# Values of the second and third attention group projected in natural token order, ahead of the queries, and brought into dilated order through DRAM

## The chip, the cores and the metric

The program runs on one core of one Trainium2 chip. The metric is the device time of one execution in microseconds (us). Three executions of the kernel before took 1969.75, 1970.76 and 1972.15 us (median 1970.76).

## What is computed

One layer of a hybrid decoder, for a prompt of 1024 tokens and for 8 decode tokens with the same weights: an input projection `h @ w_in`, a dilated attention of three head groups, a retention of four heads, gates, an output projection and a feed-forward block. The change touches the dilated attention of the prompt. Cut to that:

```python
DILATED_PATTERNS = ((128, 1), (512, 4), (2048, 16))      # (window, dilation) of the three groups
h = x * (1 + scale1) + shift1
qa, ka, va, ... = split(h @ w_in)                        # va: 3 groups x 4 heads x 64 = 3 x 256 columns
for g, (window, dil) in enumerate(DILATED_PATTERNS):
    o, lse = _dilated_group_prompt(qa[g], ka[g], va[g], window, dil)   # tokens i and j meet only if i % dil == j % dil
    keep = min(window, 1024)
    outputs += [ka[g][-keep:], va[g][-keep:]]            # prompt_k, prompt_v, in token order
```

The outputs `prompt_k` and `prompt_v` hold the last 128, 512 and 1024 tokens of the three groups, in natural token order.

## The kernel before, in words

`h` lies transposed in SBUF as eight pairs of tiles `h_hi` and `h_lo` (128 features x 1032 tokens each, `hT`), so that a product in nearly full precision is made of three matmuls: hi by hi, lo by hi, hi by lo. Two helpers project it.

`dense` (L195, matmuls in `mm3`, L191 to L193) makes queries and keys: the weights stand still and up to 384 tokens move, for four weight tiles of 128 columns in a group (two of queries, two of keys). For each of three token chunks VectorE then rotates and writes the result (L382 to L390); in the second and third group the write puts the tokens into dilated order.

`form_a` (L337, matmuls at L357 to L359) makes values: here a block of 128 tokens of `h` stands still and the 256 weight columns move. It makes eight blocks of 24 matmuls, in four pairs, each evacuated by ScalarE (L362). Which tokens form a block is told by `tok_ap` (L408): in the first group 128 neighbours, in the second every fourth token (of half the sequence), in the third every eighth. So the two later groups load the stationary operand with a step of 4 or 8 elements, and the values come out in dilated order. Ahead of the eight blocks, 8 small matmuls project the decode tokens (L345).

The loop over the groups (L372) runs: queries and keys, values, then eight blocks of attention (L430 to L475: scores on TensorE, masked maximum on VectorE, exponentials on ScalarE, transposes L462 and their copy L464, the product with V at L471), then the outputs `prompt_k` and `prompt_v`. Weights are loaded on SP's queue (`dma_w`, L174) through a ring of three buffers and split in hi and lo by ScalarE and VectorE (L154, L155). Most other transfers are issued by POOL (`dma_o`): `dq` (decode queries, keys, values), `dx` (row maxima and sums, L489), `NBt` and `Lt` (read back from `dx`), `prompt_k`, `prompt_v`. Tiles live in 34 equal slots that are given out first in, first out.

A scheduler fixes the order of each engine's instructions when the program is built: it fills the attention blocks of one group with matmuls of whatever projection the program has next. In the kernel before that is the next group's queries (or, after the third group, the retention's queries and keys); all engines and queues run their own list strictly in order.

Of the kernel before, what the change touches and what calls it, by code (L numbers as in the profile page):

```python
# [12 lines left out]
F32 = mybir.dt.float32  # L13
# [7 lines left out]
S = 1024  # L21
# [12 lines left out]
C_QA, C_KA, C_VA, C_RQ, C_RK, C_RV, C_RG, C_GA, C_GB = (  # L34
    0, 768, 1536, 2304, 2816, 3328, 4352, 5376, 6400)
# [69 lines left out]
def tile_hybrid_decoder_step(ctx: ExitStack, tc: tile.TileContext, a, o):  # L105
    nc = tc.nc
    dma_w = nc.sync
    dma_o = nc.gpsimd
# [5 lines left out]
    dram = ctx.enter_context(tc.tile_pool(name="scratch", bufs=1, space=bass.MemoryType.DRAM))  # L114
    wk_ctx = tc.tile_pool(name="work", bufs=1)
    wk = wk_ctx.__enter__()
    slots = Slots()
# [219 lines left out]
    def form_a(c0, tok_ap, out_v, dec_dram, scale=None):  # L337
        w = []
        ps = dbank((128, 256))
        for kh in range(2):  # L340
            hi, lo, raw = wload(w_in[512 * kh:512 * kh + 512, c0:c0 + 256].rearrange("(k p) c -> p k c", p=128),
                                (128, 4, 256), with_raw=True)
            w.append((hi, lo))
            for k in range(4):
                nc.tensor.matmul(ps[32 * k:32 * k + NB], hd[:, 4 * kh + k, :], raw[:, k], start=kh == 0, stop=kh == 1)  # L345
        dl = wk.tile([NB, 256], F32, tag="kk", name="dl", bufs=2)
        nc.scalar.copy(dl[:], ps[0:NB])
        for g in range(1, 4):
            nc.vector.tensor_add(dl[:], dl[:], ps[32 * g:32 * g + NB])
        dma_o.dma_start(dec_dram, dl[:])  # L350
        for pr in range(4):
            ps = dbank((128, 2, 256))
            for j in range(2):
                for k in range(8):
                    whi, wlo = w[k // 4][0][:, k % 4, :], w[k // 4][1][:, k % 4, :]
                    xh, xl = tok_ap(hT[k][0], 2 * pr + j), tok_ap(hT[k][1], 2 * pr + j)
                    nc.tensor.matmul(ps[:, j, :], xh, whi, start=k == 0, stop=False)  # L357
                    nc.tensor.matmul(ps[:, j, :], xl, whi, start=False, stop=False)  # L358
                    nc.tensor.matmul(ps[:, j, :], xh, wlo, start=False, stop=k == 7)  # L359
            dst = out_v[pr // 2][:, 2 * (pr % 2):2 * (pr % 2) + 2, :]  # L360
            if scale is None:
                nc.scalar.copy(dst, ps)  # L362
            else:
                nc.scalar.activation(dst, ps, AF.Identity, scale=scale)
    dma_o.dma_start(cst[:], a["consts"])
    dq = dram.tile([3, NB, 768], F32, name="dq")
    dx = dram.tile([3, 36, S], F32, name="dx")
    dw = dram.tile([3, 4, S], F32, name="dw")
    shuf = [8, 9, 10, 11, 12, 13, 14, 15, 0, 1, 2, 3, 4, 5, 6, 7] + list(range(16, 32))

    OG = []
    for g, (win, dil) in enumerate(PATTERNS):  # L372
        ls = min(dil, 8)
        qk = []
        for c0 in (C_QA, C_KA):
            for p in range(2):
# [35 lines left out]
                return x[:, :S].rearrange("p (b i r) -> p b r i", b=2, r=4)[:, bi % 2, bi // 2, :]  # L412
            return x[:, :S].rearrange("p (v j) -> p j v", j=8)[:, bi]

        V = [slots.alloc((128, 4, 256), name="V") for _ in range(2)]
        form_a(C_VA + 256 * g, tok_ap, V, dq[2, :, 256 * g:256 * g + 256])
        for n_, src in enumerate((qT, kT)):
            pq = bbank((NB, 2, 128))
            for p in range(2):
# [10 lines left out]
        for bi in range(8):  # L430
# [10 lines left out]
            for h in range(4):  # L441
                p, hh = h // 2, h % 2
                r = slice(64 * hh, 64 * hh + 64)
                nc.tensor.matmul(sb[hh][:, p, :nk], qT[p][r, 128 * bi:128 * bi + 128],  # L444
                                 kT[p][r, k0:k0 + nk], start=True, stop=True)
            for h in range(4):
                p, hh = h // 2, h % 2
                t = wk.tile([128, 256], F32, tag="pm", name="pm", bufs=5)
# [9 lines left out]
            for q0 in range(0, ntr, 4):  # L458
                pb = bbank((128, 4, 128))
                for j in range(4):  # L460
                    h, b = divmod(q0 + j, len(kb))
                    nc.tensor.transpose(pb[:, j, :], pm[h][:, 128 * b:128 * b + 128], ident[:])  # L462
                t = wk.tile([128, 4, 128], F32, tag="PT", name="PT", bufs=2)
# [3 lines left out]
            for h in range(4):  # L467
                p, hh = h // 2, h % 2
# [24 lines left out]
        blks = {1: [7], 4: [1, 3, 5, 7], 16: list(range(8))}[dil]  # L493
        ko, vo = o["prompt_k%d" % g], o["prompt_v%d" % g]
        if dil > 1:
            ko, vo = [t.rearrange("(i r) c -> i r c", r=ls) for t in (ko, vo)]
        for b0 in range(0, len(blks), 4):
            part = blks[b0:b0 + 4]
            kk = slots.alloc((128, 4, 256), name="kout")
            for j in range(0, len(part), 2):  # L500
                two = part[j:j + 2]
                pk = bbank((128, 2 * len(two), 128))
                for i, bi in enumerate(two):
                    for p in range(2):
                        nc.tensor.transpose(pk[:, 2 * i + p, :], kT[p][:, 128 * bi:128 * bi + 128], ident[:])
                nc.scalar.copy(kk[:, j:j + len(two), :].rearrange("p a (b c) -> p (a b) c", b=2), pk)
            if dil == 1:
                dma_o.dma_start(ko, kk[:, 0])
                dma_o.dma_start(vo, V[1][:, 3])
            elif dil == 4:  # L510
                dma_o.dma_start(ko, kk[:])
                for i in range(2):
                    dma_o.dma_start(vo[:, 2 * i:2 * i + 2], V[i][:, 1::2])
            else:
                dma_o.dma_start(ko[:, b0:b0 + 4], kk[:])
                dma_o.dma_start(vo[:, b0:b0 + 4], V[b0 // 4][:])
            slots.free(kk)
        slots.free(*qk, *V)

# [146 lines left out]
    for h in range(4):  # L666
# [21 lines left out]
        if h == 3:  # L688
            slots.free(rc, rs)
        dv = dram.tile([NB, 256], F32, name=f"dv{h}")  # L690
        form_a(C_RV + 256 * h, lambda x, bi: x[:, 128 * bi:128 * bi + 128], V, dv[:],
               scale=vs[:, h:h + 1])
        gt = [slots.alloc(name="gated") for _ in range(2)]
        gated += gt
# [17 lines left out]
        for c in range(8):  # L712
            cs_ = slice(128 * c, 128 * c + 128)
            v = V[c // 4][:, c % 4, :]
# [423 lines left out]
```

## Time and profile before

| | |
|---|---|
| executions | 1969.75, 1970.76, 1972.15 us |
| span of the profiled execution | 1970.4 us (its time with what lies around the span was not recorded separately) |
| TensorE busy, matmuls | 1924.3 us, 98% |
| TensorE busy, weight loads | 1815.7 us, 92% |
| VectorE, ScalarE, GpSimd busy | 793.9, 550.9, 229.3 us |
| DMA | 217.21 MB, mean 110 GB/s |
| granted TensorE clock, mean | 0.995 |

The matmuls overlap in the profile: each lasts longer than the distance to the start of the next, so a busy TensorE is not one without slack. The distance from start to start tells what a matmul costs.

### The profile page before, as it was taken

To read this page: it belongs to the slowest core of one execution; us is meant where nothing else is said; L and a number is where in the kernel's file an instruction comes from. 1 tells how busy PE (TensorE), PEld (TensorE's weight loads), DVE (VectorE), ACT (ScalarE), POOL (GpSimd) and SP (SyncE) were. 2 spreads that over 40 slices of the span, in tenths; PEclk is the share of its full clock that TensorE was granted. 3 is DMA by queue.
4 is the path that set the end of the run, shared out by engine and by line. 5 is a ranking of instruction groups with operands and counts; after the bars stand their busy time and mean duration, and the time that the engine had idled before them with its cause. 6 is when DMAs were issued, how large, how long until landed. Compare 5 with 4: busy or idle time off the path is not lost.

```text
span 1970.4 us, 29739 instructions
## 1 busy us (share of the span) xinstructions
PE 1924.3 (98%) x12406; PEld 1815.7 (92%) x12406; DVE 793.9 (40%) x1824; ACT 550.9 (28%) x1118; POOL 229.3 (12%) x310
## 2 busy tenths in 40 slices
PE   7999999999999999999999999999999999999996
PEld 5879979889998998888999989999999999999996
DVE  4736153377644341211165366221133323323338
ACT  3251140424243342112132454212221112111212
POOL 2000000032000000000001553000000000000015
PEclk9999999999999999999999999999999999999998
DMA  9301101185223143334211554223343534444332
GB/s 273 105 25 33 50 26 44 55 238 166 76 68 100 56 134 106 112 113 129 63 56 56 173 169 137 76 75 109 110 166 129 183 128 154 139 137 139 107 108 86
DMA packets 209080, 217.21 MB, mean 110 GB/s; under 512 B 7621, under 2 KB 185133, under 8 KB 208178
## 3 DMA queue, kind: packets, MB, share of 16 engines
q1 hardware_dynamic: 190962, 117.50, 20.8%
q0 software_dynamic: 17856, 97.72, 13.9%
q8 instruction: 97, 1.59, 0.3%
q14 instruction: 37, 0.30, 0.0%
q10 hardware_dynamic: 128, 0.10, 0.0%
HBM read 193.88 MB, written 65.45 MB: 132 GB/s over the span
## 4 chain that ended last, share of the span: by engine, by line
PE 85%; issue 4%; DVE 4%; DMA 3%; ACT 2%; POOL 1%; SPq 1%; DVEq 0%; POOLq 0%; ACTq 0%
PE ps_d L191 22%; PE ps_d L192 22%; PE ps_d L193 22%; PE ps_d L357 3%; PE ps_d L359 3%; PE ps_d L358 3%; PE ps_a L224 2%; PE ps_a L444 1%; DMA qb<-dq 1%; PE ps_b L462 1%; PE ps_o L471 1%; POOL w_lo L155 1%; DMA vb<-dv 1%; DVE h_lo L155 1%; DMA wb<-dw 1%
## 5 line engine op out<-in xcount | busy, mean ns | idle before, releaser
L191 PE MATMUL ps_d<-h_hi,w_hi 128*128 128x384 f32 (+3 forms) x2064 | 667.1, 323 | 0.6 <-ACT tm L1015 0.6
L192 PE MATMUL ps_d<-h_lo,w_hi 128*128 128x384 f32 (+3 forms) x2064 | 663.5, 321 | 0.0
L193 PE MATMUL ps_d<-h_hi,w_lo 128*128 128x384 f32 (+3 forms) x2064 | 662.2, 321 | 0.0
L191 PEld LDWEIGHTS ps_d<-h_hi,w_hi 128*128 128x128 f32 x2064 | 388.3, 188 | 23.7 <-issue 17.6
L193 PEld LDWEIGHTS ps_d<-h_hi,w_lo 128*128 128x128 f32 x2064 | 388.3, 188 | 2.8 <-issue 2.3
L192 PEld LDWEIGHTS ps_d<-h_lo,w_hi 128*128 128x128 f32 x2064 | 388.3, 188 | 2.6 <-issue 1.8
L155 DVE TENSOR_TENSOR w_lo<-w_raw,w_hi 128x1024 fp32r<-128x1024 f32 (+2 forms) x140 | 158.4, 1132 | 387.2 <-ACT w_hi L154 386.5
L154 ACT CAST w_hi<-w_raw 128x1024 fp32r<-128x1024 f32 (+2 forms) x164 | 161.7, 988 | 471.9 <-PE ps_d L192 397.6
L1018 DVE TENSOR_TENSOR tm<-tm,ps_d 128x392 f32<-128x392 f32 (+2 forms) x66 | 33.9, 513 | 272.0 <-PE ps_d L193 270.5
L357 PE MATMUL ps_d<-w_hi,h_hi 128*128 128x256 f32 x448 | 141.6, 316 | 0.0
L359 PE MATMUL ps_d<-w_lo,h_hi 128*128 128x256 f32 x448 | 140.9, 315 | 0.7 <-DVE w_lo L155 0.7
L358 PE MATMUL ps_d<-w_hi,h_lo 128*128 128x256 f32 x448 | 140.8, 314 | 0.0
L191 PE MATMUL ps_d<-ff_hi,w_hi 128*128 128x384 f32 (+1 forms) x432 | 138.3, 320 | 0.0
L193 PE MATMUL ps_d<-ff_hi,w_lo 128*128 128x384 f32 (+1 forms) x432 | 138.1, 320 | 0.0
L192 PE MATMUL ps_d<-ff_lo,w_hi 128*128 128x384 f32 (+1 forms) x432 | 138.1, 320 | 0.0
L357 PEld LDWEIGHTS ps_d<-w_hi,h_hi 128*128 128x128 f32 x448 | 102.9, 230 | 3.0 <-issue 2.6
L359 PEld LDWEIGHTS ps_d<-w_lo,h_hi 128*128 128x128 f32 x448 | 103.0, 230 | 0.9 <-DVE w_lo L155 0.9
L358 PEld LDWEIGHTS ps_d<-w_hi,h_lo 128*128 128x128 f32 x448 | 103.1, 230 | 0.0
L168 POOL COPY tick<-tk 1x1 f32<-1x1 f32 x54 | 10.9, 202 | 706.3 <-DVE tk L167 706.3
L154 ACT CAST ff_hi<-tm 128x392 fp32r<-128x392 f32 (+2 forms) x66 | 31.6, 479 | 187.8 <-DVE tm L1018 187.8
L191 PEld LDWEIGHTS ps_d<-ff_hi,w_hi 128*128 128x128 f32 x432 | 81.2, 188 | 0.0
L192 PEld LDWEIGHTS ps_d<-ff_lo,w_hi 128*128 128x128 f32 x432 | 81.1, 188 | 0.0
(324 smaller groups left out, 2722.0 us busy)
## 6 DMA issues: line engine op xcount, KB each, us to landing
w_raw<-w_in SPq DMA_DIRECT2D x56, 512.0 KB, 4.3
w_raw<-w_ffn_in SPq DMA_DIRECT2D x44, 512.0 KB, 3.9
ada_raw<-w_ada SPq DMA_DIRECT2D x32, 512.0 KB, 4.2
sample_k<-cache_k POOLq DMA_DIRECT2D x8, 2047.0 KB, 10.2
sample_v<-cache_v POOLq DMA_DIRECT2D x8, 2047.0 KB, 9.3
w_raw<-w_o SPq DMA_DIRECT2D x24, 512.0 KB, 3.8
w_raw<-w_ffn_out SPq DMA_DIRECT2D x24, 384.0 KB, 3.4
ada_raw<-w_ada SPq DMA_DIRECT2D x32, 256.0 KB, 5.7
```

Source lines behind the costliest of these rows:

```text
L154: nc.scalar.copy(hi, raw)
L155: eng.tensor_sub(lo, raw, hi.bitcast(F32))
L191: nc.tensor.matmul(ps, whi[:, k0 + k, :], xhi[:, t0:t0 + n], start=f, stop=False)
L192: nc.tensor.matmul(ps, whi[:, k0 + k, :], xlo[:, t0:t0 + n], start=False, stop=False)
L193: nc.tensor.matmul(ps, wlo[:, k0 + k, :], xhi[:, t0:t0 + n], start=False, stop=l)
L224: nc.tensor.matmul(ps[32 * g:32 * g + 32], cs[:, k0 + k, :], w[:, k], start=k0 + k < 4, stop=k0 + k >= 4)
L357: nc.tensor.matmul(ps[:, j, :], xh, whi, start=k == 0, stop=False)
L358: nc.tensor.matmul(ps[:, j, :], xl, whi, start=False, stop=False)
L359: nc.tensor.matmul(ps[:, j, :], xh, wlo, start=False, stop=k == 7)
L444: nc.tensor.matmul(sb[hh][:, p, :nk], qT[p][r, 128 * bi:128 * bi + 128], kT[p][r, k0:k0 + nk], start=True, stop=True)
L462: nc.tensor.transpose(pb[:, j, :], pm[h][:, 128 * b:128 * b + 128], ident[:])
L1018: nc.vector.tensor_mul(tm[:, :n], tm[:, :n], pu)
```

## The change

For the second and third group (`dil > 1`) a new function `values` runs at the head of the loop's body, ahead of the queries. It projects the values with `natural` blocks (128 neighbouring tokens) into two new tiles `Vn`, writes them by POOL's queue to a DRAM tile `vx` (1024 x 256), writes `prompt_v` from the same tiles, and reads `vx` back by SP's queue into the tiles `V` in dilated order. The attention reads `V` as before. The first group keeps its place and form.

```diff
+    def natural(x, bi):
+        return x[:, 128 * bi:128 * bi + 128]
+
+    def values(g, dil):
+        N = [slots.alloc((128, 4, 256), name="Vn") for _ in range(2)]
+        form_a(C_VA + 256 * g, natural, N, dq[2, :, 256 * g:256 * g + 256])
+        vo = o["prompt_v%d" % g]
+        vx = dram.tile([S, 256], F32, name=f"vx{g}")
+        for i in range(2):
+            rows = vx[512 * i:512 * i + 512].rearrange("(b p) c -> p b c", p=128)
+            dma_o.dma_start(rows, N[i][:])
+        for i in range(2):
+            r0 = 512 * i - S + vo.shape[0]
+            if r0 >= 0:
+                dma_o.dma_start(vo[r0:r0 + 512].rearrange("(b p) c -> p b c", p=128), N[i][:])
+        slots.free(*N)
+        V = [slots.alloc((128, 4, 256), name="V") for _ in range(2)]
+        for i in range(2):
+            if dil == 4:
+                for b in range(2):
+                    dma_w.dma_start(V[i][:, b::2], vx[512 * b:512 * b + 512]
+                                    .rearrange("(i r) c -> i r c", r=4)[:, 2 * i:2 * i + 2])
+            else:
+                dma_w.dma_start(V[i][:], vx.rearrange("(v j) c -> v j c", j=8)[:, 4 * i:4 * i + 4])
+        return V
+
     OG = []
     for g, (win, dil) in enumerate(PATTERNS):
         ls = min(dil, 8)
+        if dil > 1:
+            V = values(g, dil)
...
-        V = [slots.alloc((128, 4, 256), name="V") for _ in range(2)]
-        form_a(C_VA + 256 * g, tok_ap, V, dq[2, :, 256 * g:256 * g + 256])
+        if dil == 1:
+            V = [slots.alloc((128, 4, 256), name="V") for _ in range(2)]
+            form_a(C_VA + 256 * g, natural, V, dq[2, :, 256 * g:256 * g + 256])
...
             elif dil == 4:
                 dma_o.dma_start(ko, kk[:])
-                for i in range(2):
-                    dma_o.dma_start(vo[:, 2 * i:2 * i + 2], V[i][:, 1::2])
             else:
                 dma_o.dma_start(ko[:, b0:b0 + 4], kk[:])
-                dma_o.dma_start(vo[:, b0:b0 + 4], V[b0 // 4][:])
```

The order of the instructions moves at three places. In the lists below the changed kernel's lines from L371 on stand 26 to 29 lower than the same lines before (scores L444 become L473, transposes L462 become L491, the product with V L471 becomes L500).

The first place is TensorE at the start of the first group's attention. Before, the fillers between its matmuls are the second group's queries:

```order
L444 MATMUL ps_a<-qk_701,qk_663 128x128 x2
L444 MATMUL ps_a<-qk_801,qk_682 128x128 x2
L191 MATMUL ps_d<-h_hi_176,w_hi 128x384
L192 MATMUL ps_d<-h_lo_177,w_hi 128x384
L193 MATMUL ps_d<-h_hi_176,w_lo 128x384
L191 MATMUL ps_d<-h_hi_234,w_hi 128x384
```

And in the changed kernel:

```order
L473 MATMUL ps_a<-qk_701,qk_663 128x128 x2
L473 MATMUL ps_a<-qk_801,qk_682 128x128 x2
L345 MATMUL ps_d<-w_raw,hd 8x256 x8
L357 MATMUL ps_d<-w_hi,h_hi_176 128x256
L473 MATMUL ps_a<-qk_701,qk_663 128x256 x2
L473 MATMUL ps_a<-qk_801,qk_682 128x256 x2
L358 MATMUL ps_d<-w_hi,h_lo_177 128x256
L359 MATMUL ps_d<-w_lo,h_hi_176 128x256
```

The fillers are now the second group's values; its queries and keys follow when the values are done. The same holds one group on: the third group's values fill the second group's attention. Between the first score and the last product with V of an attention stand 56 dense matmuls before and 48 of values now (first group), 62 and 75 (second group), 48 and 59, dense both times (third group); 8 of L345 come on top in the first two.

The second place is POOL's queue from the end of the first group's attention (`dx`, `NBt`, `Lt`) to the decode keys `dq` of the second group, in the changed kernel:

```order
L518 DMA dx<-X_1146 36x1024
L537 DMA prompt_k<-kout_1509 128x256
L550 DMA NBt<-dx 128x32
L551 DMA Lt<-dx 128x32
L381 DMA vx_1745<-Vn_1516 128x4x256
L381 DMA vx_1745<-Vn_1517 128x4x256
L385 DMA prompt_v<-Vn_1517 128x4x256
L452 DMA dq<-tk 8x256 x2
```

The two writes of `vx` and the one of `prompt_v` are new here; two half as large writes of `prompt_v` stood behind the values before.

The third place is SP's queue, which held nothing but weights here before. In the changed kernel (`w_raw` of 128x4x256 are weights of values, two for a group; of 128x8x128 those of queries and keys, four for a group, then those of the retention):

```order
L391 DMA V_81_1749<-vx1_1745 128x2x256
L391 DMA V_82_1750<-vx1_1745 128x2x256
L174 DMA w_raw_2524<-w_in 128x4x256
L174 DMA w_raw_2534<-w_in 128x4x256
...
L174 DMA w_raw_3547<-w_in 128x8x128
L174 DMA w_raw_3650<-w_in 128x8x128
L394 DMA V_93_2755<-vx2_2750 128x1024
L394 DMA V_94_2756<-vx2_2750 128x1024
L174 DMA w_raw_3793<-w_in 128x4x256
L174 DMA w_raw_3803<-w_in 128x4x256
```

The second group's reads of `vx` stand behind the weights of its own queries and keys, and ahead of the third group's weights (two of the four reads behind the first two of them); the third group's reads stand behind its queries and keys and the retention's first two weights, ahead of the retention's values.

## Rows read from the trace of the kernel before

**Rows 1.** The page: busy time of TensorE, and its granted clock in 40 slices

```profile
PE 1924.3 (98%) x12406; PEld 1815.7 (92%) x12406; DVE 793.9 (40%) x1824; ACT 550.9 (28%) x1118; POOL 229.3 (12%) x310
...
PEclk9999999999999999999999999999999999999998
```

**Rows 2.** Stretches: busy PE, PEld, DVE, ACT, POOL (instructions); granted clock; DMA share; GB/s

```profile
112.00:157.00 45.00, 44.76 (x320) 31.22 (x319) 24.53 (x103) 28.17 (x84) 1.57 (x3) 1.00 0.10 27
...
192.00:237.00 45.00, 45.00 (x207) 44.22 (x206) 4.26 (x11) 4.17 (x6) 1.28 (x2) 1.00 0.15 42
237.00:281.00 44.00, 43.29 (x307) 31.69 (x307) 23.61 (x102) 25.80 (x85) 2.29 (x4) 1.00 0.10 31
281.00:315.00 34.00, 34.00 (x219) 34.00 (x218) 22.46 (x52) 3.36 (x4) 1.64 (x3) 1.00 0.12 37
...
420.00:460.00 40.00, 36.80 (x231) 34.51 (x230) 30.79 (x45) 12.18 (x28) 11.71 (x17) 0.91 0.88 269
```

**Rows 3.** TensorE in order of time: first values matmul of each group, first matmul behind them

```profile
88.42 1.05 PE L345 MATMUL ps_d<-w_raw,hd 128*8 128x256 f32 x16
89.41 0.39 PE L357 MATMUL ps_d<-w_hi,h_hi 128*128 128x256 f32 x1
...
112.09 0.38 PE L420 MATMUL ps_b<-ident,qk 128*8 128x128 f32 x2
...
193.62 0.51 PE L357 MATMUL ps_d<-w_hi,h_hi 128*128 128x256 f32 x1
...
238.85 0.60 PE L420 MATMUL ps_b<-ident,qk 128*8 128x128 f32 x4
...
316.22 0.51 PE L357 MATMUL ps_d<-w_hi,h_hi 128*128 128x256 f32 x1
...
362.71 0.60 PE L420 MATMUL ps_b<-ident,qk 128*8 128x128 f32 x4
```

**Rows 4.** Weight loads of L357 by group (first, second, third): busy us, mean ns

```profile
L357 PEld LDWEIGHTS ps_d<-w_hi,h_hi 128*128 128x128 f32 x64 | 12.0, 188 | 0.4 <-DVE t L383 0.4
...
L357 PEld LDWEIGHTS ps_d<-w_hi,h_hi 128*128 128x128 f32 x64 | 21.2, 331 | 0.4 <-issue 0.4
...
L357 PEld LDWEIGHTS ps_d<-w_hi,h_hi 128*128 128x128 f32 x64 | 21.6, 338 | 0.4 <-issue 0.4
```

**Rows 5.** Groups of instructions of 112 to 157 us: busy, mean ns, idle before

```profile
L454 ACT ACTIVATE pm<-pm,st 128x256 f32<-128x256 f32 (+1 forms) x32 | 15.4, 484 | 8.1 <-DVE st L452 8.0
...
L390 DVE TENSOR_TENSOR qk<-t,sh 128x384 f32<-128x384 f32 x2 | 1.7, 832 | 0.0
L382 DVE STREAM_SHUFFLE sh<-ps_d 128x384 f32<-128x384 f32 x2 | 1.2, 590 | 0.0
L384 DVE TENSOR_TENSOR sh<-sh,rope_s 128x384 f32<-128x384 f32 x2 | 1.1, 547 | 0.0
L383 DVE TENSOR_TENSOR t<-ps_d,rope_c 128x384 f32<-128x384 f32 x2 | 1.1, 545 | 0.0
```

**Rows 6.** TensorE, 115 to 117 us: start, duration of dense fillers behind scores

```profile
115.80 0.44 PE L191 MATMUL ps_d<-h_hi,w_hi 128*128 128x384 f32 x1
116.08 0.34 PE L192 MATMUL ps_d<-h_lo,w_hi 128*128 128x384 f32 x1
116.26 0.34 PE L193 MATMUL ps_d<-h_hi,w_lo 128*128 128x384 f32 x1
```

**Rows 7.** ScalarE in order of time: the copy of a values block pair

```profile
106.65 0.59 ACT L362 COPY V<-ps_d 128x512 f32<-128x512 f32 x1 [5.05 <-PE ps_d L359]
```

**Rows 8.** DMA issues: KB each, median us from issue to landing

```profile
w_raw<-w_in SPq DMA_DIRECT2D x56, 512.0 KB, 4.3
...
qb<-dq POOLq DMA_DIRECT2D x6, 512.0 KB, 11.6
...
prompt_v<-V POOLq DMA_DIRECT2D x2, 512.0 KB, 3.9
```

**Rows 9.** What TensorE waited for, 400 to 520 us: total, times, longest

```profile
PE ps_b L701 <- ACT kt L707: 3.6, 2, 3.2
```

More of the change, by code (lines that the diff above doesn't have):

```diff
@@ L495, in tile_hybrid_decoder_step @@
         if dil > 1:
-            ko, vo = [t.rearrange("(i r) c -> i r c", r=ls) for t in (ko, vo)]
+            ko = ko.rearrange("(i r) c -> i r c", r=ls)
         for b0 in range(0, len(blks), 4):
@@ L690, in tile_hybrid_decoder_step @@
         dv = dram.tile([NB, 256], F32, name=f"dv{h}")
-        form_a(C_RV + 256 * h, lambda x, bi: x[:, 128 * bi:128 * bi + 128], V, dv[:],
+        form_a(C_RV + 256 * h, natural, V, dv[:],
                scale=vs[:, h:h + 1])
```

## The prediction, made before the changed kernel was run

> **What bounds the kernel now.** I read the page first: TensorE is busy 98% of the span at a granted clock of nearly full speed throughout, the other engines 40% at most [rows 1]. Since busy matmuls overlap, that alone doesn't tell whether TensorE is the bound, so I then read the stretches of the three groups: while values are projected, matmuls and weight loads are both busy all the time (192 to 237 us) and VectorE works 4 us of 45; in the attention stretches (112 to 157, 237 to 281 us) weight loads are busy only 31 us of 45, so there is some slack there [rows 2]. A microsecond taken from the projections of values should therefore come out of the total, if nothing new makes TensorE wait. Transfers are few in these stretches (DMA share 0.10 to 0.15); they crowd later, at 420 to 460 us (0.88) [rows 2].
>
> **The part that pays: the step in the stationary operand.** The three projections of values are alike but for the order of the tokens: 192 matmuls each, 256 columns moving. The first group's run from 89.41 to 112.09 us, 22.68 us or 0.118 us a matmul; the second's from 193.62 to 238.85, 45.23 us or 0.236; the third's from 316.22 to 362.71, 46.49 us or 0.242 [rows 3]. The clock is full in the second (1.00 from 192 to 237 us) [rows 2], so this is not the clock. [...] With natural blocks in all groups each projection should take the first group's 22.68 us: 45.23 - 22.68 = 22.55 and 46.49 - 22.68 = 23.81, in all **46.4 us less**.
>
> [...]
>
> **What is added, and what hides it.**
> - *The round trip.* For each group two writes of `vx` of 512 KB (POOL), and reads of 1 MB in all (SP); `prompt_v` is written from other tiles but is no larger than before. Behind the last values matmul come ScalarE's copy, 0.6 us [rows 7], the last write, 3.9 us as the `prompt_v` of that size takes, and two reads, 4.3 us each as weights of that size take on the same queue [rows 8]: 13 us if the reads don't overlap. No row shows a read of DRAM just written; the slowest transfer of that size takes 11.6 us [rows 8], and with that price for all three the trip is 0.6 + 3 x 11.6 = 35.4 us. The cover is the group's own queries and keys: 4 weight tiles x 72 matmuls = 288, at 34.00 / 219 = 0.155 us (281 to 315 us, nothing else runs there) [rows 2], 44.7 us. Even the dear end fits, so I take 0. Were the cover gone, the trip would cost its 13 us in each group.
> - *SP's queue.* The reads wait for the writes, and the weights behind them wait too: the third group's behind the second group's reads, the retention's values behind the third's. Those are wanted only when 288 matmuls are done, and the queries' and keys' weights stand ahead of the reads. 0 for the same cover.
> - *POOL's queue.* The writes of `vx` stand behind `NBt` and `Lt`, which wait for `dx` of the attention before. That attention ends while the values are still being projected (of 192 values matmuls 48 to 75 lie inside it), so the wait is over before `Vn` is complete. 0. What stands behind the writes (`dq`) has nobody waiting for it for the next 100 us.
> - *ScalarE and VectorE.* The four copies of values, the decode copy with its three small adds and the splits of the weights are moved, not added. VectorE's rotation is moved out of the attention stretches (next point).
> - *Slots.* Two more are held in a group; the queries' tiles now take slots of the attention just ended, whose reads are over when the queries run. 0.
>
> **The attention stretches, with other fillers.** In the first two attentions the fillers change from dense matmuls, 0.175 us each in a row and 0.28 us where they follow other work [rows 6], to values, 0.118 us. TensorE has waits of its own there; how many grow is not shown by any row, so I bound them. Dear end: both stretches last as long as before although their fillers are worth less. First group: 56 x 0.175 = 9.8 us of work before, now 48 x 0.118 = 5.7 plus 1.0 us of L345 (89.41 - 88.42 in the first group) [rows 3], 3.1 us lost; second group: 62 x 0.175 = 10.9 against 75 x 0.118 + 1.0 = 9.9, 1.0 lost; together +4.1. Cheap end: the exponentials waited 8.0 us for VectorE in the first stretch, and VectorE spent 5.1 us there on rotating the fillers' results, which is no longer in the way [rows 5]; if each of the two stretches gets shorter by that, -10.2. The cheap end leans on a wait that TensorE feels only in part, the dear end on there being no relief; they nearly balance, and I take 0.
>
> **The sum.** 1970.4 us (span of the profiled execution) - 46.4 = 1924.0. The median of the runs shown, 1970.76, is 0.4 above that span, less than the runs differ among themselves; I keep **1924 us**.
>
> **Rivals.**
> - *The attentions wait more* (dear end above): 1924 + 4.1 = **1928**. For: fewer matmuls between dependent steps. Against: VectorE is freed at the same time.
> [...]
> - *The trip is late, a little*: each lands 10 us behind its cover (55 us in all): 1924 + 20 = **1944**. Against: even the dear end of 35.4 us fits.
> - *The trip is late, much, and the change is slower.* SP's queue stands still on the reads, TensorE on V at the first product of the second and third attention. This decides from a trip of 44.7 + 46.4 / 2 = 68 us on; at 72 us each the time would be 1924 + 2 x 27.3 = **1979**. No transfer of this size comes near.
> - *The step is not the cause*: the second and third group are slow for a reason that the change leaves, and nothing is gained: **1970**. [...]
>
> **How the numbers follow.** The forecast (both projections at 22.7 us, trip hidden, attention stretches within a few us) 0.66; the attentions wait more 0.15; the later stall goes or doubles 0.12; trip a little late 0.03; much late 0.02; step not the cause 0.02. Predicted is the likeliest, 1924. The range takes in the bounds of the attention stretches (1914 to 1928) and a later stall that doubles on top of the dear end (1928 + 6.8 = 1935): 1914 to 1936. Only the last three cases lie outside it, and what I have not thought of. With over 0.2% (3.9 us, about what runs of this kernel can tell from no change) as the line, faster has all cases but two: 0.96; the step's case is the same, 0.02; much late is slower, 0.02.
>
> **What would show it right or wrong.** Right: loads of L357 near 188 ns in all groups and no values matmul 0.24 us behind the last; the reads of `vx` landing some 13 us after the last values matmul, some 30 us before the attention; no wait of TensorE for V at L500 (L471 before); the later stretches the same, 46 us earlier. Wrong: loads of 331 ns on natural blocks (then the step was not it), TensorE idle at L500 or at the third group's L345 behind a DMA (trip late), or attention stretches of more than 45 and 43 us at the same work (fillers).

## The result and the profile after

The changed kernel took 1927.04 us (median of four executions, 1924.57 to 1931.34), the kernel before beside it 1971.45 us (1969.75 to 1973.21): a ratio of 0.9775, 95% interval 0.9761 to 0.9789, or 44.4 us less. The forecast was 1924, its range 1914 to 1936. Timed twice more, each time beside the kernel before, the changed kernel took 1923.25 us (ratio 0.975, 0.9737 to 0.9763) and 1924.49 us (0.9761, 0.9747 to 0.9774); how far one program varies is told below.

The page of the changed kernel shows TensorE still busy 98%, of a span that is 43.3 us shorter, at nearly the same granted clock (mean 0.994, before 0.995) [rows 1]:

```profile
span 1927.1 us, 29754 instructions
...
PE 1879.8 (98%) x12406; PEld 1770.6 (92%) x12406; DVE 793.9 (41%) x1824; ACT 551.3 (29%) x1118; POOL 233.1 (12%) x313
...
PEclk9999999999999999999999999999999999999998
```

The weight loads of all values, those of the retention among them, now have one mean duration, in the groups of instructions of TensorE's load port; before it was 188, 331 and 338 ns by group [rows 4]:

```profile
L357 PEld LDWEIGHTS ps_d<-w_hi,h_hi 128*128 128x128 f32 x448 | 84.3, 188 | 3.6 <-issue 3.1 <-DVE t L411 0.4
```

TensorE in order of time [rows 3]: the first group's values start at 88.76 us and end before 111.45; the second's first and last matmul are at 113.60 and 171.10, the third's at 219.32 and 273.70, and the second and third attention (L473) begin at 216.79 and 319.39.

```profile
88.76 0.39 PE L357 MATMUL ps_d<-w_hi,h_hi 128*128 128x256 f32 x1
...
111.45 0.60 PE L449 MATMUL ps_b<-ident,qk 128*8 128x128 f32 x4
...
113.60 0.39 PE L357 MATMUL ps_d<-w_hi,h_hi 128*128 128x256 f32 x1
...
171.10 0.28 PE L359 MATMUL ps_d<-w_lo,h_hi 128*128 128x256 f32 x1
...
216.79 0.60 PE L473 MATMUL ps_a<-qk,qk 64*128 64x128 f32 x6
...
219.32 0.38 PE L357 MATMUL ps_d<-w_hi,h_hi 128*128 128x256 f32 x1
...
273.70 0.28 PE L359 MATMUL ps_d<-w_lo,h_hi 128*128 128x256 f32 x1
...
319.39 0.49 PE L473 MATMUL ps_a<-qk,qk 64*128 64x128 f32 x4
```

The stretches after (columns as in [rows 2]) are the first attention, the second group's queries and keys, the second attention, the third group's queries and keys. Between the attentions TensorE has no gap; inside them it has: 0.78 us of 41, and 1.32 us of 40, where before it was 0.24 of 45 and 0.71 of 44.

```profile
112.00:153.00 41.00, 40.22 (x310) 26.11 (x310) 19.95 (x93) 28.07 (x84) 2.08 (x4) 1.00 0.16 43
171.00:217.00 46.00, 46.00 (x297) 45.73 (x297) 30.00 (x66) 5.24 (x6) 1.51 (x2) 1.00 0.22 70
217.00:257.00 40.00, 38.68 (x299) 26.87 (x298) 19.81 (x97) 22.57 (x79) 1.57 (x3) 1.00 0.14 41
274.00:319.00 45.00, 45.00 (x289) 44.98 (x289) 29.15 (x63) 4.58 (x5) 1.52 (x2) 1.00 0.34 106
```

### The time by stage, for all profiles

The stages run between starts of matmuls: the first score of each attention, the first product of the retention's first block (L701 before, L727 after: "first intra"), and the last matmul of the program. An attention's *own* time runs from its first score to its last product with V, less its fillers at their distance in a row (0.1745 us a dense matmul, 0.121 a short one of 264 columns, 0.1175 one of values, 0.0615 each of the 16 matmuls that the trace records at L345). It says what the attention costs beyond the work of others inside it. All in us; the labels are those of the experiments below (e1 has no own time for two attentions, as its fillers are dilated values).

| profile | to att. 1 | att. 1 to 2 | att. 2 to 3 | to first intra | rest | own 1 | own 2 | own 3 |
|---|---|---|---|---|---|---|---|---|
| before | 112.62 | 126.76 | 123.86 | 70.30 | 1526.57 | 33.25 | 27.60 | 21.00 |
| after | 111.98 | 104.81 | 102.60 | 70.15 | 1527.10 | 34.14 | 30.42 | 21.12 |
| e1 | 112.38 | 125.90 | 124.15 | 70.12 | 1518.25 | | | 21.09 |
| e2 | 112.20 | 104.21 | 102.12 | 71.74 | 1527.55 | 33.24 | 29.68 | 22.56 |
| e3 | 112.42 | 104.37 | 102.19 | 70.16 | 1526.36 | 33.72 | 30.05 | 21.13 |
| e4 | 111.94 | 104.11 | 100.27 | 70.10 | 1525.86 | 33.24 | 27.89 | 21.07 |
| e5 | 112.35 | 104.70 | 111.40 | 70.30 | 1529.80 | 33.25 | 27.93 | 21.01 |
| e6 | 111.95 | 103.87 | 101.19 | 70.12 | 1522.91 | 33.20 | 29.01 | 21.09 |
| e7 | 113.46 | 104.12 | 100.27 | 70.12 | 1523.22 | 33.25 | 27.91 | 21.09 |
| e8 | 112.39 | 104.16 | 102.73 | 71.96 | 1521.74 | 33.51 | 30.57 | 21.08 |
| e9 | 114.01 | 103.87 | 101.18 | 70.15 | 1518.56 | 33.19 | 28.99 | 21.12 |
| after again | 111.75 | 104.18 | 102.53 | 70.13 | 1520.78 | 33.51 | 30.37 | 21.09 |
| after third | 112.17 | 104.34 | 102.59 | 70.16 | 1522.50 | 33.67 | 30.41 | 21.12 |
| before again | 112.53 | 126.76 | 123.85 | 70.30 | 1524.19 | 33.25 | 27.59 | 21.00 |

The change took 21.95 us (126.76 - 104.81) and 21.26 us (123.86 - 102.60), 43.2 us, against 46.4 forecast. The first and second attention's own times grew by 0.9 and 2.8 us, so the other work of the two stages gave its 46 us and the attentions took some 3 to 4 back. The first attention's loss varies between executions (0.9, 0.3 and 0.4 us in the three profiles of the changed kernel), the second's hardly (2.8 in each).

### Where the attentions wait now

ScalarE, first attention and second, and below them POOL and TensorE (the views in order of time of each engine):

```profile
115.52 0.36 ACT L347 COPY dl<-ps_d 8x256 f32<-8x256 f32 x1 [2.45 <-DMA dq<-tk]
115.89 1.28 ACT L483 ACT_TABLE_LOAD   x1
...
222.06 0.36 ACT L347 COPY dl<-ps_d 8x256 f32<-8x256 f32 x1 [4.56 <-PE ps_d L357]
222.33 0.40 ACT L483 ACTIVATE pm<-pm,st 128x128 f32<-128x128 f32 x1
...
218.30 0.53 POOL L452 DMA_DIRECT2D dq<-tk  x1 [43.66 <-DVE tk L451]
219.59 0.54 POOL L452 DMA_DIRECT2D dq<-tk  x1 [0.76 <-DVE mx L478]
...
222.87 0.33 PE L491 MATMUL ps_b<-ident,pm 128*128 128x128 f32 x1 [0.85 <-ACT pm L483]
```

`dl` (L347) is the copy of the decode values. It stands on ScalarE's list ahead of the first exponentials (L483), since the values now fill the attention. `dl` shares a ring of two buffers (tag "kk") with `tk`, the decode queries and keys that were written just before, so it waits until POOL's transfer `dq<-tk` has read its buffer: 2.45 us in the first attention. In the second the profile names TensorE, but the matmuls that `dl` reads (L345) were done by 219.4 us; the transfer issued at 218.30, which lands at 221.9, is what was still under way. The exponentials, their transposes and the products with V stand behind that copy. In the kernel before `dl` came ahead of `tk`, and its seven copies together waited 0.2 us.

### The round trip

The tile V after: issues of the reads and their time to land.

```profile
L391 SPq DMA_DIRECT2D V<-vx x4: 366/369/463, 164.4 to 179.2; - x4
L394 SPq DMA_DIRECT2D V<-vx x2: 345/379/413, 280.6 to 281.0; - x2
...
DMA to landing us min/median/max: 3.8/5.3/5.4
```

Behind the last values matmul (171.10 and 273.70 us) the last read is issued at 179.2 and 281.0 and lands at most 5.4 us later: 184.6 and 286.4, a trip of about 13 us in both groups, some 32 us ahead of the attentions (216.79, 319.39). TensorE waits for V nowhere at L500.

### The profile page after: what moved, and what is told of

The parts are those of the page before. It is cut to its first block, busy times and chain, and to the rows that moved or that the text cites. A ratio compares the mean times of both kernels' runs of the same rounds, so it can differ in the third digit from the quotient of the medians.

```text
span 1927.1 us, 29754 instructions
## 1 busy us (share of the span) xinstructions
PE 1879.8 (98%) x12406; PEld 1770.6 (92%) x12406; DVE 793.9 (41%) x1824; ACT 551.3 (29%) x1118; POOL 233.1 (12%) x313
## 3 DMA queue, kind: packets, MB, share of 16 engines
q1 hardware_dynamic: 192338, 119.60, 21.7%
## 4 chain that ended last, share of the span: by engine, by line
PE 88%; DVE 4%; DMA 3%; ACT 2%; issue 2%; SPq 1%; POOL 1%; DVEq 0%; POOLq 0%; ACTq 0%
PE ps_d L191 24%; PE ps_d L192 23%; PE ps_d L193 23%; PE ps_d L359 2%; PE ps_d L357 2%; PE ps_d L358 2%; DMA w_raw<-w_in 2%; PE ps_a L224 2%; PE ps_a L473 2%; PE ps_b L491 1%; PE ps_o L500 1%; DMA vb<-dv 1%; PE ps_o L745 1%; PE ps_a L747 1%; DVE h_lo L155 1%
## 5 line engine op out<-in xcount | busy, mean ns | idle before, releaser
L359 PE MATMUL ps_d<-w_lo,h_hi 128*128 128x256 f32 x448 | 127.0, 284 | 0.7 <-DVE w_lo L155 0.7
L357 PE MATMUL ps_d<-w_hi,h_hi 128*128 128x256 f32 x448 | 127.4, 285 | 0.0
L358 PE MATMUL ps_d<-w_hi,h_lo 128*128 128x256 f32 x448 | 126.2, 282 | 0.0
L357 PEld LDWEIGHTS ps_d<-w_hi,h_hi 128*128 128x128 f32 x448 | 84.3, 188 | 3.6 <-issue 3.1
L359 PEld LDWEIGHTS ps_d<-w_lo,h_hi 128*128 128x128 f32 x448 | 84.3, 188 | 2.7 <-issue 1.9
L358 PEld LDWEIGHTS ps_d<-w_hi,h_lo 128*128 128x128 f32 x448 | 84.4, 188 | 0.9 <-issue 0.7
```

## The experiments

### e1: the new place alone

Values ahead of the queries, but with the old dilated blocks straight into V, and no trip through DRAM.

```diff
-        N = [slots.alloc((128, 4, 256), name="Vn") for _ in range(2)]
-        form_a(C_VA + 256 * g, natural, N, dq[2, :, 256 * g:256 * g + 256])
...
+        form_a(C_VA + 256 * g, dilated(dil), V, dq[2, :, 256 * g:256 * g + 256])
```

> Values of the second and third group ahead of the queries as in the changed kernel, but projected in dilated order as before, straight into V: no vx, no round trip. If the step in the stationary operand is what cost (theory), the loads of L357 in these groups stay at 331 to 338 ns, both projections take 45 to 46 us of TensorE again, and with the other fillers' small loss the time is 1970 to 1976 us. If the new place ahead of the queries (other fillers, VectorE freed in the attention stretches) is what gained (rival), it stays near 1927, at most 1945.

Measured: 1964.91 us, ratio 0.9975 (0.9959 to 0.999), below the 1970 to 1976 expected. The two stages keep their times (125.90 and 124.15 against 126.76 and 123.86), so the place gives 0.6 us and the step in the stationary operand the rest. The 8 us that this kernel is shorter come from behind the first intra (1518.25 against 1526.57), where in its profile TensorE stands for only 0.7 us at the first intra and the clock stays full (1.00 from 425 to 465 us; on the mean of the execution 0.997, before 0.995); see below.

### e2: the natural order alone, at the old place

```diff
-        if dil > 1:
-            V = values(g, dil)
...
+        else:
+            V = values(g, dil)
```

> Natural order and the round trip, but at the old place, behind the keys, so that the attention begins at once behind the values and the cover of the queries and keys is gone. In the changed kernel the second group's last read of vx landed some 13 us after its last values matmul, and the first product with V comes some 8 us after the first score, so about 5 us should be exposed in each group, as TensorE waiting for V at L500. The attention stretches have their old dense fillers again, which gives back some 4 us. Theory: 1927 + 10 - 4 = 1933, between 1928 and 1945. Rival (the trip is short enough to hide anywhere, the place does not matter): 1923 or less. Rival (a read of DRAM just written is slow and only the cover hid it): over 1950.

Measured: 1930.27 us, ratio 0.9786 (0.9763 to 0.9808), which can't be told from the changed kernel's. Without the cover the trip does show, in what TensorE waited for from 105 to 360 us:

```profile
PE ps_o L500 <- DMA V<-vx: 2.8, 2, 1.5
```

And TensorE in order of time, the product that waited in the second attention:

```profile
227.34 0.66 PE L500 MATMUL ps_o<-PT,V 128*64 128x128 f32 x6 [1.27 <-DMA V<-vx]
```

It is 1.3 and 1.5 us a group, not the 13 us that the prediction put on a trip without cover: the attention begins with scores, in the second its first products (from 222.69 us) need one half of V, and those that waited stand 11 us behind its first score (216.4). In the third the first products waited, 11 us behind the first score as well (329.24 and 318.5 us). By stage the natural order alone, at the old place, gives 22.6 and 21.7 us. From the first attention to the first intra e2 takes 278.07 us against 276.84 to 277.56 in the three profiles of the changed kernel: the cover, bought with the new place, is worth some 1 us in all.

### e3: no round trip

The attention reads the natural tiles as if they were V, so its values are those of other tokens.

```diff
-        vx = dram.tile([S, 256], F32, name=f"vx{g}")
...
-        slots.free(*N)
...
-        return V
+        return N
```

> The changed kernel without the round trip: the attention reads the natural tiles Vn themselves, so the products with V pair each probability with the value of another token (that part of the computation is left out), vx is neither written nor read. Theory (trip wholly hidden by the queries and keys): the same time, 1924 to 1930. Rival (the trip costs through the queues or the DMA share): faster by what it costs, under 1922.

Measured: 1926.44 us, ratio 0.9762 (0.9742 to 0.9782), like the changed kernel's. The two stages are 0.4 us shorter each than after, and within 0.4 us of its two later profiles; the own times of the attentions stay high (33.72, 30.05). The trip is hidden, and it is not what the attentions lost their time to.

### e4: values between the queries and the keys

```diff
-        if dil > 1:
-            V = values(g, dil)
...
+            if c0 == C_KA and dil > 1:
+                V = values(g, dil)
```

> The values of the second and third group between their queries and their keys. The attention stretches are filled with dense matmuls of the queries as before the change, the cover of the trip is halved to the keys alone, 22 us against a trip of 13. Theory (the 3 us by which the change fell short of 46.4 were lost in the first two attention stretches to the weaker fillers): both stretches go back to their old length for the same filler work, no wait for V, and the time is 1921 to 1925. Rival (the shortfall lies elsewhere): 1926 to 1930, no better than the changed kernel. Rival (half the cover is too little): over 1932, with TensorE waiting at L500.

Measured: 1926.14 us, ratio 0.9771 (0.9752 to 0.9791). The fillers are queries again, `dl` is out of the attentions, and their own times are back at 33.24 and 27.89. From the first attention to the third it is 204.38 us against 207.41 after, 3.0 less, and 2.3 less than in "after again": the theory's part, by stage. The median is the rival's, 1926.14 and not 1921 to 1925: it can't tell 3 us, as the rest of the program varies by more.

### e5: other steps

The kernel before, with blocks of every second token in the second group and every third in the third.

```diff
-        form_a(C_VA + 256 * g, tok_ap, V, dq[2, :, 256 * g:256 * g + 256])
+        step = (1, 2, 3)[g]
+        form_a(C_VA + 256 * g, lambda x, bi: x[:, 64 * bi:64 * bi + 127 * step + 1:step], V,
+               dq[2, :, 256 * g:256 * g + 256])
```

> The kernel before, with the stationary operand of the values taken with step 2 in the second group (was 4) and step 3 in the third (was 8); the values are then those of other tokens, everything else is as before. It asks what the load's duration hangs on. Steps 1, 4 and 8 took 188, 331 and 338 ns in the kernel before. If the load grows with the step up to a limit, step 2 lies between (some 235 to 260 ns) and step 3 above it (280 to 300 ns). If any step but 1 costs the whole price, both take 331 ns and the projections keep their 45.2 and 46.5 us. [...] Start to start of a values matmul: 0.118 us at 188 ns, 0.236 at 331 ns; if the load sets it, 0.118 + (load - 188 ns) x 0.118 / 143 ns between them. Time, at 192 matmuls a group: between 1924 us (both as cheap as step 1) and 1971 us (both as dear as before).

Weight loads of L357 in this kernel, second group and third (columns as in [rows 4]):

```profile
L357 PEld LDWEIGHTS ps_d<-w_hi,h_hi 128*128 128x128 f32 x64 | 12.6, 196 | 0.4 <-issue 0.4
...
L357 PEld LDWEIGHTS ps_d<-w_hi,h_hi 128*128 128x128 f32 x64 | 16.8, 263 | 0.4 <-issue 0.4
```

By step the load is 188 (1), 196 (2), 263 (3), 331 (4) and 338 ns (8). From the first values matmul to the last (191 distances) it is 23.04 us or 0.121 us each at step 2, and 33.53 or 0.176 at step 3. So step 2 is nearly free (8 ns more than step 1), 3 costs half of the price (75 of 143 ns), and from 4 to 8 little is added (7 ns). That is neither of the two cases expected: step 2 lies under the 235 to 260 ns of the first and step 3 under its 280 to 300, and neither is at the 331 ns of the second. Why the load's time goes with the step in this way is not shown.

The one execution took 1940.61 us; its rest of the program (1529.80) is 3.2 us longer than before.

### e6: the decode copy in a ring of its own

The changed kernel, with the copy `dl` of the attention groups in another ring ("R"), which only the retention uses later.

```diff
-        dl = wk.tile([NB, 256], F32, tag="kk", name="dl", bufs=2)
+        dl = wk.tile([NB, 256], F32, tag="kk" if scale is not None else "R", name="dl",
+                     bufs=2 if scale is not None else 3)
```

> The changed kernel, with the decode copy of the values (L347) put in a ring of its own in place of the one that it shares with the decode keys' tile tk. Theory: in the changed kernel this copy stands ahead of exponentials on ScalarE and waits for the transfer that still reads tk, 2.5 us in the first attention and 4.6 us in the second, and that is where the attentions lost their 0.9 and 2.8 us. Then the copy waits for less than 0.5 us here, the first two attentions' own times go from 34.14 and 30.42 back to about 33.25 and 27.9 us, and the time is 1.5 to 3.5 us shorter than the changed kernel's, about 1924. Rival: the shorter fillers themselves cost it (less work of TensorE between dependent steps, as in the prediction's dear end); then the own times stay at 34 and 30 and the time at 1927.

ScalarE in order of time, first and second attention:

```profile
113.72 0.36 ACT L348 COPY dl<-ps_d 8x256 f32<-8x256 f32 x1 [0.68 <-PE ps_d L345]
...
218.48 0.36 ACT L348 COPY dl<-ps_d 8x256 f32<-8x256 f32 x1 [1.95 <-PE ps_d L345]
```

The copy now waits only for its own matmuls, and runs 1.8 us earlier in the first attention (113.72 for 115.52) and 2.6 us earlier in the second (2.7 us behind its first score, 5.3 before). Own times: 33.20 and 29.01, against 34.14 and 30.42 after. The first attention has its loss back, the second half of it. The other 1.4 us stay with the new place, where the rival has them; which part of the place costs them is not shown. The copy no longer does: the exponentials behind it now wait for VectorE (0.56 us, at 219.40), and TensorE's list of waits (0.15 us and more) is empty in both attentions. The time, 1922.25 us (ratio 0.975, 0.9737 to 0.9763), can't be told from the 1923.25 of the changed kernel beside it; nor is it clearly 1.5 to 3.5 us shorter as expected; the traces show 1.6 us (205.06 from attention 1 to 3, against 206.71 in "after again").

### e7: the crowd of transfers moved

e4, and the decode attention one retention head later.

```diff
-DEC = ((0, 1, 2), (0,))
+DEC = ((1, 2), (0, 1))
```

> The kernel with the values between the queries and the keys, and besides that the decode attention of the second and third group behind the first retention head; its loads of cached values (qb, kc and their like) then leave the crowd of transfers at the first intra. Theory: the stall at the first intra (2.9 to 4.5 us) and the 6.8 us of half clock behind it come from that crowd, and were the 8 us by which the kernel with the values ahead in dilated order gained; without the crowd there is neither, and the time is 7 to 8 us shorter than 1926, about 1918. Rival: the crowd is only moved, to the second retention head, and stalls TensorE there; then the time stays within 3 us of 1926. Second rival: the half clock comes whether TensorE stalls there or not; then only the 3 us of the stall go, 1923.

Measured: 1919.73 us, ratio 0.9733 (0.9719 to 0.9747). It is 3.5 us under the changed kernel beside it (the intervals overlap), and 6.4 under e4, from which it differs in this edit alone, but which was timed beside other runs; 7 to 8 were expected there. So the time came out near the theory, but the mechanism isn't shown: its profile, of the slowest of its four executions (1923.40 us), still waits 2.2 us at the first intra, with the clock at half for 3.4 us after it (0.87 on the mean of 387 to 397 us, 0.96 from 397 to 407).

### e8: fewer transfers in the crowd

The changed kernel without 8 of the decode attention's 12 loads of 512 KB; the decode scores of two groups are made from the first group's tiles instead.

```diff
-                kt = slots.alloc((128, 4, 256), name="kc")
-                qb = slots.alloc((128, 4, 256), name="qb")
...
+        for half in range(2):
+            kt = slots.alloc((128, 4, 256), name="kc")
+            qb = slots.alloc((128, 4, 256), name="qb")
...
+            for g in range(3):
```

> The changed kernel without 8 of the 12 loads of 512 KB (cached keys and decode queries of the second and third group) that stand in the crowd of transfers at the first intra; the decode scores of those groups are then worked out again on the first group's tiles, so VectorE's work stays and the decode outputs are not the layer's. Theory: the stall at the first intra (3.9 us in the changed kernel's first profile, 1.6 us in its second) comes from a retention weight that lands late in that crowd, and the half clock behind it comes with the stall. Then TensorE waits less than 1 us there, there is no half clock, and the executions lie closer together at the low end of the changed kernel's 1921.6 to 1931.3 us: about 1919 to 1922. Rival: the stall hangs on VectorE's and ScalarE's work there, which stays: then it is 1.6 to 3.9 us again, and the time 1923 to 1927.

Measured: 1926.25 us, ratio 0.9768 (0.9755 to 0.9781): not shorter. From 320 to 420 us TensorE waited for:

```profile
PE ps_d L357 <- ACT rV L364: 1.6, 1, 1.6
PE ps_b L727 <- ACT kt L733: 0.8, 1, 0.8
```

The stall at the first intra is small and the clock stays full (1.00 from 380 to 420 us), as the theory has it, but a new wait stands just before it: ScalarE's `rV` (scaled values of the retention), itself 16.8 us late behind VectorE (L570), whose decode work is now done at another time. The time is 4 to 7 us over what was forecast, and the run doesn't settle what the crowd costs. Its clock also falls for 3.4 us near 1098 us, far behind the crowd.

### e9: two edits together, and the changed kernel a third time

e6 with the `DEC` line of e7.

> Two edits together, each tried alone: the decode copy of the values in a ring of its own (1.0 us less than the changed kernel beside it) and the decode attention one retention head later (1919.73 with the values between queries and keys, against 1926.14 without). If they add up, the time is 1917 to 1920 us, below both parts. If the later decode attention meets another head's transfers when the program stands 2 us elsewhere, the time is that of the first alone, 1922.

> The changed kernel again, to have it timed beside these two: 1921.6 to 1931.3 us. Its profile shows either a stall of about 4 us at the first intra with 6.8 us of half clock behind it, or one of under 2 us without.

Measured: 1920.0 us (1918.75 to 1922.13), ratio 0.9735 (0.9722 to 0.9749), and 1924.49 us for the changed kernel beside it. The 4.5 us less equal the two differences beside the changed kernel, 1.0 and 3.5, but that isn't proof that they add up: neither is clear of noise, e7 had its values elsewhere, which also took the copy out of the attentions, and e9 is no faster than e7, as it was expected to be. By ratio e9 and e7 are equal, the two fastest that were found. In the third profile of the changed kernel TensorE waits 0.4 us at the first intra and the clock stays full there (1.00 from 380 to 420 us), the second of the two cases expected.

### The changed kernel and the kernel before, profiled again

> The changed kernel as it is, to have it timed beside the three others: 1924.6 to 1931.3 us, median 1927.

> The kernel before, profiled a second time. Its first profile has a stall of 3.2 us at the first intra and 6.8 us of half clock behind it; the changed kernel has had that in one profile of three (3.9 us and 6.8 us; then 1.6 and 0.4 us without half clock). If the stall belongs to the kernel before and the change only lets it come more seldom, it is here again, at a time of 1970 to 1974 us; if it comes and goes in both kernels alike, it may be missing, and the time is then 1966 to 1969 us.

Measured: 1923.25 us after again, below the 1924.6 to 1931.3 expected; 1972.37 us before again, against 1970.18 for the same kernel beside it, a ratio of 1.0014 (1.0003 to 1.0025). So two timings of one program can differ by 2 us with an interval that leaves out 1. In the kernel before the stall is here again, the first of the two cases expected. Around the first intra the three kernels' stretches read (columns as in [rows 2]), with below each what TensorE waited for there; first after, then after again, then before again:

```profile
380.00:420.00 40.00, 35.71 (x219) 32.90 (x217) 31.99 (x52) 14.03 (x32) 11.71 (x17) 0.91 0.87 268
...
PE ps_b L729 <- ACT kt L733: 3.9, 1, 3.9
```

```profile
379.00:419.00 40.00, 38.33 (x257) 34.61 (x256) 35.27 (x65) 16.40 (x35) 14.16 (x21) 1.00 0.91 288
...
PE ps_b L727 <- ACT kt L733: 1.6, 1, 1.6
```

```profile
425.00:465.00 40.00, 37.50 (x242) 34.23 (x241) 33.16 (x63) 16.10 (x35) 12.51 (x19) 0.96 0.90 288
...
PE ps_b L701 <- ACT kt L707: 2.5, 1, 2.5
```

`kt` is ScalarE's copy of the transposed keys of a retention block. What ScalarE waited for there tells why it is late; after, and then before again:

```profile
ACT w_hi L154 <- DMA w_raw<-w_in: 5.0, 1, 5.0
```

```profile
ACT w_hi L154 <- DMA w_raw<-w_in: 3.0, 1, 3.0
```

In after again ScalarE has no wait for `w_raw` there, and begins the same split 5.6 us earlier. ScalarE in order of time, after and then after again:

```profile
394.25 1.04 ACT L154 CAST w_hi<-w_raw 128x1024 fp32r<-128x1024 f32 x1 [4.98 <-DMA w_raw<-w_in]
```

```profile
388.67 1.05 ACT L154 CAST w_hi<-w_raw 128x1024 fp32r<-128x1024 f32 x1 [0.36 <-PE ps_d L358]
```

So the same program stalls in one execution and hardly in another: a retention weight lands late among other transfers, ScalarE stands on splitting it, `kt` is behind that, and TensorE waits. The other profiles agree: in the seven where ScalarE waits for `w_raw` there (before, before again, after, e2 to e5: 3.0 to 7.5 us) TensorE waits for `kt` 2.4 to 7.0 us, in the other seven 0.4 to 2.2. Why it lands late in some executions is open.

The stall is not all that differs. Matmul by matmul, the first profile of after falls 4.5 us behind the second between 390 and 415 us, and another 1.7 us at 1101, far from any of this. There TensorE had waited 1.7 us in both, at the same transpose, L952; then the clock fell to half (0.50 from 1101 to 1103 us) for 3.4 us in the first and not in the second (TensorE in order of time and the stretch behind it, after and then after again):

```profile
1099.38 0.66 PE L952 MATMUL ps_b<-ident,x 8*128 8x8 f32 x8 [1.69 <-DVE x L911]
...
1101.00:1105.00 4.00, 4.00 (x18) 4.00 (x18) 2.58 (x10) 0.89 (x8) 1.56 (x1) 0.68 0.30 77
```

```profile
1093.94 0.66 PE L952 MATMUL ps_b<-ident,x 8*128 8x8 f32 x8 [1.70 <-DVE x L911]
...
1095.00:1099.00 4.00, 4.00 (x24) 4.00 (x24) 3.17 (x10) 1.68 (x9) 2.15 (x1) 1.00 0.23 60
```

Of the fourteen profiles only after again, e1 and e9 have no such fall there. In e7 and e9 the clock also falls for 3.4 us near 64 us, which is in their longer way to the first attention (113.46 and 114.01).

## Why the prediction was right, and where it was off

**The step.** Right in size: the loads went to 188 ns in all groups; e1 shows that the place alone gives 0.6 us, e2 that the natural order alone gives 44.3 us by stage, e5 that the load and the distance of matmuls go with the step. How a longer load stretches the distance is not shown; in the trace of before a matmul of the second group starts 0.2 us ahead of its load's end (the load and the matmul of L358, load port and matmuls in order of time), in the first group 0.07 us.

```profile
194.54 0.33 PEld L358 LDWEIGHTS ps_d<-w_hi,h_lo 128*128 128x128 f32 x1
...
194.67 0.40 PE L358 MATMUL ps_d<-w_hi,h_lo 128*128 128x256 f32 x1
```

**The round trip, SP's and POOL's queues, slots.** Right: about 13 us as forecast, landed 32 to 33 us early (30 forecast), no wait at L500, and e3 without the trip is no faster. The price of the trip without cover was wrong: 13 us in each group by the prediction, 1.3 to 1.5 us in e2, as the first products that need what lands last stand 11 us behind the first score.

**The attention stretches.** This is the term that was mis-sized: taken as 0, measured as 3.2 us by stage (46.4 - 43.2) and 3.7 us by own times. That looks like the dear end of 4.1, but the dear end's sum prices all fillers of before at 0.175 us, and 8 of the 56 and 14 of the 62 are short ones of 264 columns at 0.121: with these it is 2.7 + 0.2 = 2.9 us. So it was no bound. The second attention alone lost 2.8 us and got longer, 40.22 us from first score to last product with V where it had taken 37.67. The sign named for it, stretches of more than 45 and 43 us, didn't show it (41 and 40 us). The cheap end leaned on VectorE being freed; VectorE was less busy (19.95 us of 41 in the first stretch, before 24.53 of 45 [rows 2]), but that let TensorE gain nothing: in e6, with VectorE as free and without the wait, the first attention's own time is 33.20 for 33.25. Nor was the dear end's mechanism all of it. The step that failed is the one on ScalarE, "the decode copy with its three small adds and the splits of the weights are moved, not added": the moved copy brought a wait with it, for a buffer that is still read, ahead of the exponentials. e6 shows that some 1.7 to 2.3 us go with that wait (own times of both attentions 62.21, against 64.56 in the first profile of after and 63.88 in the second). The other 1.4 us, over the 60.85 of before, stay with the new place; that the shorter fillers cost them is likely, not shown. e4, which takes both fillers and copy out of the attentions, has it all but 0.3 us back.

**The base.** The profiled execution of after took 1928.9 us with a span of 1927.1: 1.8 us lie around the span. The sum was made against the span of before as if it were a time, and so began 1.8 us too low (one of the executions shown took 1972.15). With that and the 3.2 us mended it would give 1970.4 + 1.8 - 46.4 + 3.2 = 1929.0, for the 1928.9 of this execution. That the later timings (1923.25, 1924.49) lie on the forecast is luck: by their profiles the base and the attentions, 1.8 and 2.5 to 2.7 us too low, are made up by a rest of the program that is 4 to 6 us shorter than before, which the forecast had at no change.

**The rivals.** "The attentions wait more" (1928) is what happened in the stages. "The later stall goes or doubles" happened too, from execution to execution: the first profile of after has the stall as before, and a rest of 1527.10 us; the second hardly has it, and the rest is 1520.78. With the later fall of the clock, at 1101 us, that is nearly all of the 6.3 us between them, which are more than the medians 1927.0, 1923.3 and 1924.5 differ. It isn't the change's doing alone: in the kernel before the rest was 1526.57 and 1524.19. Whether the change lets the stall come more seldom is open: a wait of over 2 us and the fall of the clock behind it were in both profiles of before and in one of the three of after, and those are few. The 6.8 us that the range adds for a stall that doubles are an estimate, the wait of 3.2 us [rows 9] and 0.09 x 40 us of clock [rows 2]; no run shows that sum, and what the profiles showed in its place are waits for `kt` of 0.4 to 7.0 us and a rest of the program of 1518.25 to 1529.80 us. Trip late, and step not the cause, are excluded by e3 and by e1 with e2.

## What to carry to other kernels

Here a stationary operand taken with a step of 4 or 8 doubled the distance of matmuls (0.236 and 0.242 us for 0.118); compare the weight loads' mean duration between places that differ in it alone. Reordering the output instead was nearly free here, with other work over the round trip: without the trip (e3) the two stages were 0.4 us shorter each at most. When a projection is moved into another stage, follow its smallest instructions as well: which buffers they share, who read those last, and what stands behind them on their engine's list. Compare stages before medians: here two executions of one program differ by more than the edits that were to be told apart, and of the two parts of this change nearly all the gain came from one, the natural order.

## What the runs showed of the hardware that was not expected

- In before and e5 the weight load of L357 (128x128 f32) grew with the step up to 4 and hardly from 4 to 8: 188, 196, 263, 331, 338 ns at steps of 1, 2, 3, 4 and 8 elements.
- After the stall at the first intra TensorE's granted clock fell to half for a while (0.50 from 394 to 400 us in after): 0.91 on the mean of the 40 us in after, 0.96 in before again, 1.00 in after again. TensorE had stood for 3.9, 2.5 and 1.6 us just before. The length of the wait alone does not tell whether it falls: after 1.7 us at L952 it fell in after and not in after again.
